# Gate and up products in one group per 512 features, with Strassen's seven products for three of eight pairs of row blocks

## The chip, the core and the metric

One core of a Trainium2 chip runs the kernel. The metric is the device time of one execution in microseconds (us). Before the change it is 1198.21 us, the median of 3 runs (1197.5 to 1198.28).

## What is computed

One encoder layer on 256 tokens of width 2048, all in 32-bit floats:

```python
u = rms_norm(h, g_mix_pre) @ w_in                       # 2048 x 5120
...                                                     # attention heads and RG-LRU heads
h = h + rms_norm(mixed, g_mix_post)
fn = rms_norm(h, g_ffn_pre)
ff = (silu(fn @ w_ffn_gate) * (fn @ w_ffn_up)) @ w_ffn_down   # 2048 x 5632, twice; 5632 x 2048
h = h + rms_norm(ff, g_ffn_post)
gate = sigmoid(rms_norm(h, g_ple_pre) @ w_ple_gate)     # 2048 x 2048
h = h + rms_norm(gate * (p @ w_ple_proj), g_ple_post)
```

The change concerns the line with `ff`: the two products of `fn` with the gate and the up weights.

## The kernel before

**Products.** A product of two 32-bit matrices is made of three matmuls. Each operand is split into a rounded high part and the rest, and high x high, high x low and low x high are added up in PSUM (lines 390, 391 and 392 of `products`). Weights come from DRAM as tiles `wr` of two row blocks (2 x 128 rows) by 512 columns, 512 KB each. ScalarE (ACT) writes the high part `wh` of a tile (`hi_stream`, line 362) and VectorE (DVE) the low part `wl` = `wr` - `wh` (`lo_stream`, line 372). TensorE (PE) then uses the tile for both halves of the tokens (t = 0, 1): 2 row blocks x 2 halves x 3 = 12 matmuls of 128 x 128 by 512 columns. The stationary operand is the transposed activation (`hT_mix_hi`, `hT_mix_lo`), one 128 x 128 block for each row block and token half.

**Segments and posts.** `seg` lists one chunk of 512 output columns. `run_seg` runs its tiles on PE into two PSUM banks (`acc`, a ring of four), and the chunk's `post` empties them. For each of the 11 blocks of 512 features there is a gate chunk (8 tiles), whose post `gate_post` lets ACT write silu into `mid`, and an up chunk (8 tiles), whose post `up_post` multiplies on DVE (line 1194), transposes the result on PE (line 262) and splits it (lines 243 and 245). The features are done in three parts of 4, 4 and 3 blocks, and after each part come four chunks of the down product. The residual `h` stays in SBUF from the mixing sub-layer to the end.

**Order.** `Plan` writes the program out in a fixed order. It holds an estimated clock for ACT, DVE, PE and the DMA queue, and with `run` it hands out the tasks that can start before PE's clock; every engine later works through its own list strictly in that order and waits on semaphores. How many weight tiles can be ahead of PE is set by the rings: `W_BUFS` = 4 split tiles, `R_BUFS` = 4 raw tiles. All loads go through the SP queue.

Of the kernel before, what the change touches and what calls it, by code (L numbers as in the profile page):

```python
# [16 lines left out]
P = 128  # L17
# [35 lines left out]
W_BUFS = 4  # L53
R_BUFS = 4
SM_BUFS = 4
LATE = 0.8

# [12 lines left out]
class Plan:  # L70
# [13 lines left out]
    def __init__(self, **slots):  # L84
        self.clk = {"act": 0.0, "dve": 0.0, "pe": 0.0, "dma": 0.0}
# [90 lines left out]
    def main(self, cost, *after):  # L176

        t = max([self.clk["pe"]] + [self.reach(e) for e in after])
        self.clk["pe"] = max(t, self.clk["pe"]) + cost
# [18 lines left out]

def dma(kb, take=None):
    return ("dma", kb / 340.0, None, take, None)  # L200
# [3 lines left out]
def layer(ctx: ExitStack, tc: tile.TileContext, a: dict, out: bass.AP):  # L204
# [5 lines left out]
    plan = Plan(wr=R_BUFS, w=W_BUFS, sm=SM_BUFS, ev=1, mid=2, bt=2)  # L210
# [4 lines left out]
    def bank(name):  # L215
        return ps.tile([P, 2, S], F32, tag="sm", name=name, bufs=SM_BUFS)

    def raw_tile():
        return wp.tile([P, 2, N], F32, tag="wr", name="wr", bufs=R_BUFS)

# [34 lines left out]
    def transposed(e, b0):  # L255

        yield pe(0.44, take="sm")
        tr = bank("tr")
        for b in range(2):
            for t in range(NT):  # L260
                sl = slice((b0 + b) * P, (b0 + b + 1) * P)
                nc.tensor.transpose(tr[:, b, t * P : (t + 1) * P], e[:, t, sl], ident)  # L262
        return tr
# [26 lines left out]
    class Act:  # L290


        def __init__(self, blocks=KD):
            self.at = {}
# [24 lines left out]

    raws, his, los = {}, {}, {}  # L320
# [4 lines left out]
    def pieces(i):  # L325

        return [slice(0, 1), slice(1, 2)] if i == 0 else [slice(0, 2)]

    def load_stream():
        for i, (w, k, n0) in enumerate(tiles):  # L330
            for j in pieces(i):
# [5 lines left out]
                if not j.start:  # L337
                    raws[i] = raw_tile()
# [3 lines left out]
    at_hi, at_lo, at_pe = [0], [0], [0]  # L342
# [5 lines left out]
    def hi_stream():  # L348
        for i in range(len(tiles)):
            at_hi[0] = i  # L350
            for j in pieces(i):
# [4 lines left out]
                yield act(n * N, take=None if j.start or i in big_w else "w")  # L356
                if i in big_w:
                    his[i], los[i] = big_w[i][0](), big_w[i][1]()
                elif not j.start:
                    his[i] = wp.tile([P, 2, N], F32R, tag="wh", name="wh")  # L360
                    los[i] = wp.tile([P, 2, N], F32R, tag="wl", name="wl")
                nc.scalar.copy(his[i][:, j, :], raws[i][:, j, :])  # L362
                done(ev_hi[i, j.stop])

    def lo_stream():
        for i in range(len(tiles)):
            at_lo[0] = i
            for j in pieces(i):
                n = j.stop - j.start
                yield ev_hi[i, j.stop]  # L370
                yield dve(n * N, give="wr" if j.stop == 2 else None)
# [5 lines left out]
            raws.pop(i)  # L377

    MM = 0.216

    def products(i, kx, lhs, accs, ts, start, stop, *after):
        for j in range(2):
            here = ev_lo[i, j + 1] if (i, j + 1) in ev_lo else ev_lo[i, 2]
            plan.main(6 * MM * len(ts) / NT, here, lhs.ev[kx + j], *after)
# [12 lines left out]

    def free_w(i):
        if i not in keep:
            plan.free["w"].append(plan.clk["pe"])  # L400

    keep = set()
    opened = []

    def open_chunk(chunk):
        if len(opened) >= 2:
            plan.reach(opened[-2].free)
        opened.append(chunk)
        chunk.accs = [ps.tile([P, N], F32, tag="acc", name=f"acc{t}") for t in range(NT)]

    def run_seg(s):
# [5 lines left out]
        for n, (_, kx) in enumerate(ks):  # L417
            i = i0 + n
            before = [opened[-3].free] if first and n == 0 and len(opened) > 2 else []
            products(i, kx, lhs, chunk.accs, range(NT), first and n == 0,  # L420
                     last and n == len(ks) - 1, *before)
# [153 lines left out]
    def evac(ch, func, tables):  # L575
# [8 lines left out]
        done(ch.free)  # L584
# [297 lines left out]
    def v_post(g):  # L882
        def post(ch):
# [14 lines left out]
            done(ch.free)  # L898
# [74 lines left out]
    def open_p2():  # L973
# [5 lines left out]
        for n in ("h", "mg", "ple"):  # L979
            t2[n] = rs.tile([P, NT, D], F32, name=n)  # L980
        t2["pTh"] = rs.tile([P, 2, S], F32R, name="pTh")
        t2["pTl"] = rs.tile([P, 2, S], F32R, name="pTl")
        t2["pw"] = rs.tile([P, 2, S], F32, name="pw")
        plan.add(load_p2(), plan.clk["pe"])

    pT = Act(2)
    ev_h = Event()
# [8 lines left out]
    def load_p2():  # L996
# [6 lines left out]
        for t in range(NT):  # L1003
            yield dma(1024)
            nc.sync.dma_start(t2["h"][:, t, :], a["x"][t * P : (t + 1) * P, :])
# [6 lines left out]
    class Sub:  # L1012
# [10 lines left out]
        def chunk(self, c, ch, add=False):  # L1023
# [28 lines left out]
            done(ch.free)  # L1052
# [9 lines left out]
        def squares(self, c, t, src, ev):  # L1062
            yield act(N)
            junk = t2["pool"].tile([P, N], F32, tag="junk", name="junk", bufs=2)
# [7 lines left out]
    def next_norm(sub, nxt, rstd, ev_rstd, g_next):  # L1072
# [11 lines left out]
        plan.add(next_gain(g_next, plan.now), plan.now)  # L1084
        yield ev_h
# [4 lines left out]
        for c in range(4):  # L1090
            if c > 1:
                yield nxt.ev[4 * c - 8]
            for b in range(2):
                sl = slice(c * N + b * S, c * N + (b + 1) * S)
                for t in range(NT):
                    yield dve(S)
                    nc.vector.scalar_tensor_tensor(
                        out=h[:, t, sl], in0=mg[:, t, sl], scalar=ro[:, t : t + 1],
                        in1=h[:, t, sl], op0=ALU.mult, op1=ALU.add,
# [3 lines left out]
        for c in range(4):  # L1103
            sl = slice(c * N, (c + 1) * N)
            for t in range(NT):
                yield act(N)
                junk = t2["pool"].tile([P, N], F32, tag="junk", name="junk", bufs=2)
                nc.scalar.activation(junk, h[:, t, sl], AF.Square, accum_out=ssh[:, t, c : c + 1])
# [4 lines left out]
        done(ev_rstd)  # L1113

# [4 lines left out]
    def transpose_h(b, hi, lo, nxt, gname):  # L1119
        tr = yield from transposed(t2["h"], b)  # L1120
        for j in range(2):
            kk = b + j
            yield from gained_split(
                hi[:, kk, :], lo[:, kk, :], tr[:, j, :], col(gname, kk), give="sm" if j else None
            )
            done(nxt.ev[kk])


    def ple_post(c):
        def post(ch):  # L1130
            for t in range(NT):
                yield act(N)
                nc.scalar.copy(t2["ple"][:, t, c * N : (c + 1) * N], ch.accs[t])
            done(ch.free)
# [40 lines left out]
    def gate_post(f):  # L1175
        def post(ch):
            yield ev_rf
            for t in range(NT):
                yield act(N, SILU, take=None if t else "mid")
                if t == 0:  # L1180
                    es[f] = t2["pool"].tile([P, NT, N], F32, tag="mid", name="mid", bufs=2)
                nc.scalar.activation(
# [243 lines left out]
```

## Time and profile before

| what | value |
|---|---|
| median of the runs | 1198.21 us |
| span of the profiled execution (first to last instruction) | 1195.1 us |
| PE busy in that span | 1176.7 us, 5388 matmuls |
| DVE busy | 695.1 us |
| ACT busy | 635.0 us |
| DMA traffic | 232.23 MB, mean 194 GB/s |

The page gives no separate time for the profiled execution. Its span is 3.1 us below the median of the runs; that difference is what lies around the span. Read the table from the top: PE's row says how much of the span the products alone take, the rows of DVE and ACT how much room is left beside them.

### The profile page before, as it was taken

How to read it: one execution, taken by the hardware profiler on the slowest of the kernel's cores; microseconds unless marked ns; L12 is line 12 of the kernel's file. 1: busy time of each engine (PE TensorE's matmuls, PEld its weight loads, DVE VectorE, ACT ScalarE, POOL GpSimd, SP SyncE). 2: the span in 40 equal slices, each digit the busy share in tenths (PEclk: the TensorE clock that was granted, in tenths of full speed). 3: DMA queues.
4: the chain of work that ended last, by engine and by line, in shares of the span. 5: the costliest groups of instructions: out<-in, count | busy, mean ns of one | idle time of the engine just before them, and what ended most of it. 6: DMA issues, size and time to landing. Idle time of an engine off the chain costs nothing.

```text
span 1195.1 us, 14294 instructions
## 1 busy us (share of the span) xinstructions
PE 1176.7 (98%) x5388; PEld 975.7 (82%) x5388; DVE 695.1 (58%) x823; ACT 635.0 (53%) x842; POOL 1.6 (0%) x13
## 2 busy tenths in 40 slices
PE   7999999999999999999999999999999999999996
PEld 5888888888888888888888888888888888888885
DVE  5676867877557545545444544545454544657664
ACT  6787776766457344344444444443334444446753
POOL 0000000000000000000000000000000000000000
PEclk9999999999999999999999999999999999999998
DMA  8765566545865666566666566565666666565661
GB/s 305 234 213 186 154 197 188 172 160 183 314 196 195 191 193 183 190 193 187 193 194 193 186 193 191 184 194 187 193 194 194 189 184 194 175 208 177 218 222 72
DMA packets 69205, 232.23 MB, mean 194 GB/s; under 512 B 7440, under 2 KB 13456, under 8 KB 68496
## 3 DMA queue, kind: packets, MB, share of 16 engines
q1 hardware_dynamic: 68992, 231.24, 61.2%
q8 instruction: 42, 0.69, 0.2%
q14 instruction: 27, 0.22, 0.1%
q10 hardware_dynamic: 144, 0.08, 0.0%
HBM read 229.19 MB, written 2.10 MB: 194 GB/s over the span
## 4 chain that ended last, share of the span: by engine, by line
PE 98%; DVE 1%; ACT 0%; DMA 0%; SPq 0%; issue 0%; DVEq 0%
PE acc L392 31%; PE acc L390 31%; PE acc L391 31%; PE tr L262 2%; DMA xs<-in_xT 0%; PE pg L267 0%; PE pg L268 0%; PE pg L266 0%; PE tr L877 0%; DVE wl L372 0%; DVE h L1310 0%; PE po L268 0%; PE sc L267 0%; PE sc L268 0%; PE po L267 0%; PE po L266 0%
## 5 line engine op out<-in xcount | busy, mean ns | idle before, releaser
L372 DVE TENSOR_TENSOR wl<-wr,wh 128x1024 fp32r<-128x1024 f32 (+1 forms) x409 | 497.2, 1221 | 379.4 <-ACT wh L362 379.1
L362 ACT CAST wh<-wr 128x1024 fp32r<-128x1024 f32 (+1 forms) x409 | 428.7, 1050 | 471.5 <-PE acc L392 451.5
L390 PE MATMUL acc<-wh,hT_mix_hi 128*128 128x512 f32 x704 | 275.8, 392 | 0.0
L392 PE MATMUL acc<-wh,hT_mix_lo 128*128 128x512 f32 x704 | 274.3, 390 | 0.3 <-DVE hT_mix_lo L251 0.3
L391 PE MATMUL acc<-wl,hT_mix_hi 128*128 128x512 f32 x704 | 274.0, 389 | 0.0
L392 PEld LDWEIGHTS acc<-wh,hT_mix_lo 128*128 128x128 f32 x704 | 132.1, 188 | 28.5 <-DVE hT_mix_lo L251 0.9
L391 PEld LDWEIGHTS acc<-wl,hT_mix_hi 128*128 128x128 f32 x704 | 132.2, 188 | 26.9
L390 PEld LDWEIGHTS acc<-wh,hT_mix_hi 128*128 128x128 f32 x704 | 132.2, 188 | 26.6
L390 PE MATMUL acc<-wh,hT_hi 128*128 128x512 f32 x320 | 127.9, 400 | 6.9 <-ACT wh L362 6.9
L391 PE MATMUL acc<-wl,hT_hi 128*128 128x512 f32 x320 | 125.7, 393 | 1.4 <-DVE wl L372 1.4
L392 PE MATMUL acc<-wh,hT_lo 128*128 128x512 f32 x320 | 125.5, 392 | 0.0
L390 PEld LDWEIGHTS acc<-wh,hT_hi 128*128 128x128 f32 x320 | 60.6, 189 | 18.5 <-ACT wh L362 6.9
L391 PEld LDWEIGHTS acc<-wl,hT_hi 128*128 128x128 f32 x320 | 60.4, 189 | 14.7 <-DVE wl L372 3.2
L392 PEld LDWEIGHTS acc<-wh,hT_lo 128*128 128x128 f32 x320 | 60.3, 189 | 12.9
L390 PE MATMUL acc<-wh,mid0h 128*128 128x512 f32 x128 | 50.0, 390 | 0.0
L390 PE MATMUL acc<-wh,mid1h 128*128 128x512 f32 x128 | 50.0, 390 | 0.0
L392 PE MATMUL acc<-wh,mid0l 128*128 128x512 f32 x128 | 49.8, 389 | 0.0
L392 PE MATMUL acc<-wh,mid1l 128*128 128x512 f32 x128 | 49.8, 389 | 0.0
L391 PE MATMUL acc<-wl,mid0h 128*128 128x512 f32 x128 | 49.8, 389 | 0.0
L391 PE MATMUL acc<-wl,mid1h 128*128 128x512 f32 x128 | 49.8, 389 | 0.0
L390 PE MATMUL acc<-wh,hT_ffn_hi 128*128 128x512 f32 x112 | 44.1, 394 | 0.0
L392 PE MATMUL acc<-wh,hT_ffn_lo 128*128 128x512 f32 x112 | 43.7, 390 | 0.0
(231 smaller groups left out, 1308.4 us busy)
## 6 DMA issues: line engine op xcount, KB each, us to landing
wr<-in_w_ffn_gate SPq DMA_DIRECT2D x88, 512.0 KB, 4.2
wr<-in_w_ffn_up SPq DMA_DIRECT2D x88, 512.0 KB, 4.2
wr<-in_w_ffn_down SPq DMA_DIRECT2D x88, 512.0 KB, 4.3
wr<-in_w_in SPq DMA_DIRECT2D x79, 512.0 KB, 4.3
wr<-in_w_out SPq DMA_DIRECT2D x32, 512.0 KB, 4.6
wr<-in_w_ple_gate SPq DMA_DIRECT2D x32, 512.0 KB, 4.2
xn<-in_x SPq DMA_DIRECT2D x4, 512.0 KB, 6.2
h<-in_x SPq DMA_DIRECT2D x2, 1024.0 KB, 8.1
```

The source lines that it names most:

```text
L262: nc.tensor.transpose(tr[:, b, t * P : (t + 1) * P], e[:, t, sl], ident)
L362: nc.scalar.copy(his[i][:, j, :], raws[i][:, j, :])
L372: nc.vector.tensor_tensor(out=los[i][:, j, :], in0=raws[i][:, j, :], in1=f32(his[i][:, j, :]), op=ALU.subtract,)
L390: nc.tensor.matmul(accs[t], hi[:, sl], wh[:, j, :], start=st, stop=False)
L391: nc.tensor.matmul(accs[t], hi[:, sl], wl[:, j, :], start=False, stop=False)
L392: nc.tensor.matmul(accs[t], lo[:, sl], wh[:, j, :], start=False, stop=sp)
```

## The change

**One group for gate and up.** For each block of 512 features the two chunks become one `Group`. It goes through the eight pairs of row blocks once, and at each pair uses the gate tile and the up tile. So it needs four banks at once: `c11`, `c21` (gate, the two token halves) and `c12`, `c22` (up).

**Plain and Strassen units.** `KINDS` = "ppspspsp" says how each pair is done: "p" is plain (two tiles, 24 matmuls), "s" is done by seven products. The first group uses `FIRST` = "ppppspsp", with two "s". In a unit "s" the 2 x 2 block product (two row blocks; two token halves; gate and up) is done by seven block products of three matmuls each, 21 in all. Three of these products add straight into `c11`, `c12` and `c21`; four have banks of their own (`p1`, `p5`, `p6`, `p7`) in which all "s" units of a group add up.

**Sums.** Seven products need sums of the operands. For the activations (`act_sums`) they are made once, for row block pairs 4, 8 and 12, and kept in `sums_f`. For the weights (`sum_stream`) DVE makes two sum tiles per unit from the raw gate and up tiles, four subtractions of 128 x 512; they lie in `lent_t`, which has two places. The sum tiles are then split into high and low like raw tiles. Of the up tile only the second row block is split. So a unit "s" splits three and a half tiles where a unit "p" splits two.

**After the products** (`Gated`): `early` runs after the last "s" unit: ACT copies `p1`, DVE makes four additions from `p6`, `p5`, `p7`, `p5`. `late` runs at the group's end: four additions of DVE onto `c11`, `c21`, `c12`, `c22`, then silu, product, transposes and split as before. The two rings of four banks, `acc` and `sm`, change roles from group to group: one holds `c..`, the other `p..`, and the transposes of `late` take their banks in the ring of the old `c..`.

**Room.** `W_BUFS` goes from 4 to 6, one more split tile follows in the second half (`W_MORE`), and `h` is lent: after its norm it is written to DRAM (`kept0`, `kept1`, 1 MB each), its place serves as one more split tile (`lent_w`) and two more raw tiles (`lent_r`), and it is read back after the last group. The place of the gain serves as `lent_t`. Besides, `junk` gets one buffer, `sg` shares the buffers of `mid`, and the planner's estimate of a matmul goes from 0.216 to 0.2267.

```diff
-W_BUFS = 4
+W_BUFS = 6
...
+MM = 0.2267
...
+FIRST = "ppppspsp"
+KINDS = "ppspspsp"
...
+    def sum_stream():
+        for i, (i0, n) in sums.items():
...
+            a_, b_ = raws[i0], raws[i0 + 1]
+            yield dve(N, take="ts")
+            raws[i] = t = from_slot("ts", i)
...
+            first = b_[:, 0, :] if not n else b_[:, 1, :]
+            minus = a_[:, 0, :] if not n else raws[i - 1][:, 0, :]
+            nc.vector.tensor_tensor(out=t[:, 0, :], in0=first, in1=minus, op=ALU.subtract)
+            yield dve(N)
+            first = b_[:, 1, :] if not n else a_[:, 1, :]
+            minus = b_[:, 0, :] if not n else t[:, 0, :]
+            nc.vector.tensor_tensor(out=t[:, 1, :], in0=first, in1=minus, op=ALU.subtract)
...
+    FORMS = (
+        ("p1", 0, 0, (0, 0)), ("c11", 0, 1, (1, 0)), ("c12", 1, 1, 3), ("p5", 2, 0, 0),
+        ("p7", 2, 1, 2), ("p6", 3, 0, 1), ("c21", 3, 1, (1, 1)),
+    )
...
+    def seven(i, kx, g, start, stop):
+        for name, v, j, which in FORMS:
+            n = i + v
...
+            own = name[0] == "p"
+            at = g.take(name) if own and start else 0.0
+            plan.main(3 * MM, ev_lo[n, 2], ev, at=at)
+            times3(g.banks[name], hi, lo, his[n][:, j, :], los[n][:, j, :],
+                   own and start, own and stop)
...
+        def early(self, g):
...
+            nc.scalar.copy(e[:, 0, :], bk["p1"])
...
+            nc.vector.tensor_tensor(out=e[:, 1, :], in0=bk["p6"], in1=e[:, 0, :], op=ALU.add)
...
+            nc.vector.tensor_tensor(out=u[0], in0=bk["p5"], in1=e[:, 1, :], op=ALU.add)
...
+            nc.vector.tensor_tensor(out=e[:, 1, :], in0=bk["p7"], in1=e[:, 1, :], op=ALU.add)
...
+            nc.vector.tensor_tensor(out=u[1], in0=bk["p5"], in1=e[:, 1, :], op=ALU.add)
...
+        def late(self, g):
...
+            for t, n, x in (
+                (0, "c11", e[:, 0, :]), (1, "c21", e[:, 1, :]), (0, "c12", u[0]), (1, "c22", u[1]),
+            ):
+                yield dve(N)
+                nc.vector.tensor_tensor(out=x, in0=bk[n], in1=x, op=ALU.add)
...
+    def lend_h(h):
...
+            nc.sync.dma_start(t2["kept"][t], h[t])
...
+    def give_back():
+        yield ev_back["w"]
+        yield ev_back["wr"]
...
+            nc.sync.dma_start(t2["h"][t], t2["kept"][t])
...
         for f in range(f0, f1):
-            g = Chunk(gate_post(f))
-            seg(g, "w_ffn_gate", f * N, hF, KS)
-            seg(Chunk(up_post(f, mid, (f - f0) * 4, g)), "w_ffn_up", f * N, hF, KS)
+            Group(("w_ffn_gate", "w_ffn_up"), (f * N, f * N), hF,
+                  [(k, k) for k in ORDER], KINDS if f else FIRST, Gated(mid, (f - f0) * 4))
```

**How the order changes.** Three places matter for the steps below. In the names, a number tells tiles of one name apart.

VectorE's list before, where the post of an up chunk falls (the third block of features): between two posts there stand only splits of weight tiles.

```order
L372 TENSOR_TENSOR wl_4118<-wr_4061,wh_4117 128x1024
L372 TENSOR_TENSOR wl_4136<-wr_4073,wh_4135 128x1024
L372 TENSOR_TENSOR wl_4154<-wr_4091,wh_4153 128x1024
L1194 SCALAR_TENSOR_TENSOR mid_4024<-acc0_4016,rstd_f_92,mid_4024 128x512
L1194 SCALAR_TENSOR_TENSOR mid_4024<-acc1_4017,rstd_f_92,mid_4024 128x512
L372 TENSOR_TENSOR wl_4175<-wr_4109,wh_4174 128x1024
L245 TENSOR_TENSOR mid0l1_4191<-tr_4185,mid0h1_4190 128x512
L372 TENSOR_TENSOR wl_4195<-wr_4127,wh_4194 128x1024
```

VectorE's list now, at the end of `late` of the second group, while PE goes through the first units of the third group (the last row, `wl_4051`, is the low part of the second sum tile of that group's first "s" unit):

```order
L1513 SCALAR_TENSOR_TENSOR mid_3920<-u_lo_3933,rstd_f_94,mid_3920 128x512
L482 TENSOR_TENSOR lent_w_3414<-lent_r_3415,lent_w_3414 128x1024
L506 TENSOR_TENSOR lent_t_3127<-lent_r_3415 128x512
L291 TENSOR_TENSOR mid0l0_3662<-tr_4002,mid0h0_3661 128x512
L482 TENSOR_TENSOR wl_3936<-lent_r_3415,wh_3935 128x512
L502 TENSOR_TENSOR lent_t_3127<-lent_r_3415,lent_t_3127 128x512
L482 TENSOR_TENSOR wl_4017<-lent_t_3127,wh_4016 128x1024
L291 TENSOR_TENSOR mid0l0_3662<-tr_4027,mid0h0_3661 128x512
L506 TENSOR_TENSOR lent_t_3127<-lent_r_3415,lent_t_3127 128x512
L502 TENSOR_TENSOR lent_t_3127<-wr_3985,wr_3962 128x512
L506 TENSOR_TENSOR lent_t_3127<-wr_3985 128x512
L482 TENSOR_TENSOR wl_4051<-lent_t_3127,wh_4050 128x1024
```

The splits of `late`, the subtractions for the sums (lines 502 and 506) and the splits of weight tiles now stand between each other; `wl_4051` stands behind two subtractions that belong to the next "s" unit.

PE's list now, at the end of the eleventh group, where the down chunk takes the two `acc` banks that `c11` and `c21` of this group held:

```order
L523 MATMUL c12_7876<-wh_8089,hT_mix_lo_3129 128x512
L521 MATMUL c22_7877<-wh_8089,hT_mix_hi_3128 128x512
L522 MATMUL c22_7877<-wl_8090,hT_mix_hi_3128 128x512
L523 MATMUL c22_7877<-wh_8089,hT_mix_lo_3129 128x512
L521 MATMUL acc0_8197<-wh_8101,mid2h0_7554 128x512
L522 MATMUL acc0_8197<-wl_8102,mid2h0_7554 128x512
```

VectorE's list before those two banks come free (lines 1484 to 1493 are `early`, line 1506 is `late`):

```order
L1484 TENSOR_TENSOR mid_8155<-p6_7981,mid_8155 128x512
L1488 TENSOR_TENSOR u_hi_8171<-p5_7969,mid_8155 128x512
L1490 TENSOR_TENSOR mid_8155<-p7_7974,mid_8155 128x512
L1493 TENSOR_TENSOR u_lo_8172<-p5_7969,mid_8155 128x512
L482 TENSOR_TENSOR wl_8161<-wr_8127,wh_8160 128x1024
L482 TENSOR_TENSOR wl_8176<-wr_8135,wh_8175 128x1024
L1506 TENSOR_TENSOR mid_8155<-c11_7853,mid_8155 128x512
L1506 TENSOR_TENSOR mid_8155<-c21_7854,mid_8155 128x512
```

Before the change PE went here from an up chunk to two other banks of the ring, which had been empty for a whole chunk; now the first two banks of the down chunk come free with the last two rows.

The SP queue now, in the first group: the two stores of `h` stand between the loads of plain tiles and the loads of the last "s" unit, which land in `h`'s place.

```order
L432 DMA wr_3341<-in_w_ffn_gate 128x1024
L432 DMA wr_3356<-in_w_ffn_up 128x1024
L1328 DMA kept0_3387<-h0_2694 128x2048
L1328 DMA kept1_3388<-h1_2695 128x2048
L432 DMA lent_r_3415<-in_w_ffn_gate 128x1024
L432 DMA lent_r_3415<-in_w_ffn_up 128x1024
```

What moved: all later loads stand behind these stores, and the two `lent_r` loads also wait until the stores have read `h`.

More of the change, by code (lines that the diff above doesn't have):

```diff
@@ L1132, in post @@
                 yield act(N)
[L1133 to L1134 removed]
+                nc.scalar.copy(ple_of(c)[:, t, :], ch.accs[t])
+            release(ch)
         return post
@@ L1326, in layer @@
                 ev[i, j.stop] = Event()
+    for i, (i0, n) in sums.items():
+        if not n:
+            for u in (i0, i0 + 1, i):
+                uses[u] += 1
     i0 = segs[-1][-1]
```

421 lines of the change are left out of this document (337 added, 84 removed).

## The prediction, made before the changed kernel was run

> **What bounds the kernel now.** I read the page first: busy times and the chain that ended last.
>
> ```profile
> span 1195.1 us, 14294 instructions
> PE 1176.7 (98%) x5388; PEld 975.7 (82%) x5388; DVE 695.1 (58%) x823; ACT 635.0 (53%) x842; POOL 1.6 (0%) x13
> ...
> PE 98%; DVE 1%; ACT 0%; DMA 0%; SPq 0%; issue 0%; DVEq 0%
> ```
>
> PE is busy 1176.7 of 1195.1 us and the chain is PE nearly from end to end. Next the list of waits, for PE alone, and the busy time from the first gate chunk to the middle of the FFN.
>
> ```profile
> PE acc L390 <- ACT wh L362: 6.9, 1, 6.9
> PE acc L391 <- DVE wl L372: 1.4, 2, 0.7
> PE acc L392 <- DVE hT_mix_lo L251: 0.3, 1, 0.3
> ...
> 360.00:728.00 368.00, 368.00 (x1657) 304.72 (x1656) 187.18 (x182) 167.69 (x195) 0.00 (x0) 1.00 0.62 191
> ```
>
> Columns of the last row: the stretch, its length, then busy time (and count) of PE, PEld, DVE, ACT, POOL, PE's granted clock, the DMA share and GB/s. PE waited 8.6 us in all, 6.9 of them for its first weights, and in the FFN not at all: 368.00 of 368.00 us, at clock 1.00. DVE is at 187.18 (51%). So there a matmul less is time less, as long as DVE, which gets much more work, keeps ahead.
>
> The price of a matmul is not its duration (they overlap) but the distance of starts:
>
> ```profile
> 700.31 0.39 PE L390 MATMUL acc<-wh,hT_mix_hi 128*128 128x512 f32 x1
> ...
> 705.75 0.39 PE L390 MATMUL acc<-wh,hT_mix_hi 128*128 128x512 f32 x1
> ...
> 540.14 0.44 PE tr L262 x4
> ```
>
> These two starts are 24 matmuls apart: 5.44 / 24 = 0.2267 us. Four transposes take 0.44.
>
> **What PE saves.** Each "s" unit has 21 matmuls for 24. There are 2 in the first group and 3 in each of ten: 32 x 3 = 96 matmuls less, 96 x 0.2267 = 21.8 us. A group takes PE 183 x 0.2267 + 2 x 0.44 = 42.4 us (before: 192 x 0.2267 + 0.88 = 44.4). [...]
>
> **What DVE and ACT get.** DVE's rows (duration in ns at the end of the busy column), ACT's and the DMA's:
>
> ```profile
> L372 DVE TENSOR_TENSOR wl<-wr,wh 128x1024 fp32r<-128x1024 f32 x407 | 495.8, 1223 | 379.4 <-ACT wh L362 379.1
> L1194 DVE SCALAR_TENSOR_TENSOR mid<-acc,rstd_f,mid 128x512 f32<-128x512 f32 x22 | 15.4, 744 | 0.0
> L1279 DVE TENSOR_TENSOR sg<-sg,ple 128x512 f32<-128x512 f32 x8 | 5.5, 688 | 11.9 <-ACT sg L1275 11.9
> L1232 DVE TENSOR_TENSOR mg<-acc,mg 128x512 f32<-128x512 f32 x8 | 5.1, 683 | 0.0
> ...
> L362 ACT CAST wh<-wr 128x1024 fp32r<-128x1024 f32 x407 | 427.5, 1052 | 471.5 <-PE acc L392 451.5 <-DMA wr<-in_w_out 5.1 <-issue 4.9
> L1182 ACT ACTIVATE mid<-acc,rstd_f 128x512 f32<-128x512 f32 x22 | 15.0, 690 | 9.9 <-PE acc L392 9.9
> L1229 ACT COPY mg<-acc 128x512 f32<-128x512 f32 x8 | 4.7, 589 | 4.3 <-PE acc L392 3.9
> ...
> wr<-in_w_ffn_gate SPq DMA_DIRECT2D x88, 512.0 KB, 4.2
> ...
> h<-in_x SPq DMA_DIRECT2D x2, 1024.0 KB, 8.1
> ```
>
> A group of five "p" and three "s" has on DVE: splits of 128 x 1024: 5 x 2 + 3 x 3 = 19; pieces of 128 x 512: 3 (half tiles) + 12 (sums) + 4 (`early`) + 4 (`late`) + 2 (splits of `mid`) = 25; 2 of line 1194's kind. By durations (L1279 and L1232 for the pieces, 0.69): 19 x 1.223 + 25 x 0.69 + 2 x 0.744 = 42.0 us. That would be PE's 42.4, with nothing to spare. But do durations add up? The timeline of DVE where it is dense:
>
> ```profile
> 362.31 1.22 DVE L372 TENSOR_TENSOR wl<-wr,wh 128x1024 fp32r<-128x1024 f32 x1
> 363.44 0.48 DVE L1097 SCALAR_TENSOR_TENSOR h<-mg,ro_mix,h 128x256 f32<-128x256 f32 x1
> ...
> 408.33 0.69 DVE L245 TENSOR_TENSOR mid0l<-tr,mid0h 128x512 fp32r<-128x512 f32 x1 [1.98 <-ACT mid0h L243]
> 408.94 1.22 DVE L372 TENSOR_TENSOR wl<-wr,wh 128x1024 fp32r<-128x1024 f32 x1
> ...
> 448.03 1.40 DVE L1194 SCALAR_TENSOR_TENSOR mid<-acc,rstd_f,mid 128x512 f32<-128x512 f32 x2
> ...
> 1123.12 0.69 DVE L1279 TENSOR_TENSOR sg<-sg,ple 128x512 f32<-128x512 f32 x1 [0.78 <-ACT sg L1275]
> 1123.85 0.69 DVE L1284 TENSOR_TENSOR mg<-sg,gain_g_ple_post 128x512 f32<-128x512 f32 x1
> ```
>
> The first columns are start and length. A next instruction starts 1.13 us after a split of 1.22, 0.61 after a piece of 0.69, 0.66 (1.40 - 0.74) after line 1194's; only where it uses the result of the one just before (L1284 after L1279) is it 0.73. So a group costs DVE 19 x 1.13 + 25 x 0.61 + 2 x 0.66 = 38.0, and about 12 dependent pairs (`early`, sums, `late`) x 0.12 = 1.4: 39.4 us, 93% of PE's 42.4. ACT has 19 x 1.05 + 3 x 0.59 + 0.59 + 2 x 0.69 + 2 x 0.59 = 24.9 us: room. Loads are the same 16 tiles per group, 8.4 MB in 42.4 us, 198 GB/s against 191 in the row above; they and the loads' issue stay hidden behind split tiles, of which seven or eight can now be ahead of PE (19 us of plain tiles at 2.72).
>
> [...]
>
> **New waits of PE, one by one.**
>
> First, the second sum tile of a group's first "s" unit. In the list shown, `wl_4051` stands behind the whole of `late`. From the group's start, DVE has up to it the four additions, 2 of line 1194's kind, 4 splits of 1024 and 8 pieces more: 12 x 0.61 + 2 x 0.66 + 4 x 1.13 = 13.2 us, with 8 dependent pairs 14.1; by durations 14.7. PE needs it after two "p" units, two transposes and five products: 48 x 0.2267 + 0.88 + 15 x 0.2267 = 15.2 us. It holds by 0.5 to 1.1 us, if no cast of ACT (1.05) that DVE waits for is exposed. One exposed in each of ten groups would cost up to 0.5 us each, two 1.6. I take 0.2 on average, 2 us; ends 0 and 16.
>
> Second, the banks. `early` has the 5.44 us of the last "p" unit: ACT's copy 0.59 and four dependent additions of 0.73 are 3.5 us. It holds by 1.9, more than one split (1.13) in the way. Then, from one group to the next, the banks of `c..` need only be free for the next "s" unit, 11 us later. But at the end of the eleventh group the down chunk takes the banks of `c11` and `c21` at once: 3.5 + two splits 2.26 + one addition 0.61 = 6.4 us after the last "s" unit, against 5.44: PE waits 1.0 us there, once. Ends 0 and 4 (ACT's copy late by one cast, three splits more). After the fourth and the eighth group the down chunk takes what were banks of `p..`, free since `early`: nothing.
>
> Third, `h` to DRAM. The last "s" unit of the first group comes 117 matmuls, 26.5 us, after the last transposes of `h`. Before its sums can be made, the SP queue must reach the stores (behind a tile whose place comes free some 6.5 us after the last rows of `h`, by DVE's list), the stores must land (8.1 us as for the two loads of `h`, if they overlap; 16.2 if not), the tiles must land (4.2), then four subtractions (2.9), a cast (1.05) and a split (1.2). That is 24 or 32 us against 26.5 plus 2 us until the first sum is used. I take 1 us, nearer the overlapped case since both loads of `h` show 8.1 with weights between them; ends 0 and 4. Coming back, `h` has the 65 us of the last down chunks: nothing. If that cover went, next late would be the norm before the PLE gate.
>
> Other edits cost nothing, all hidden behind a PE that is 98% busy: the sums of the activations (three times about 1.6 us of DVE and ACT, in the 26 us after the norm, where the first four units are plain), the one buffer of `junk` (written by ACT alone, in order), `sg` in `mid`'s place (no `mid` lives then), the larger rings. Unchanged: the start (6.9 + 1.4 us in the rows of waits) and the tail:
>
> ```profile
> 1100.00:1195.00 95.00, 85.28 (x382) 70.18 (x381) 58.52 (x76) 53.52 (x87) 0.00 (x0) 0.96 0.51 167
> ```
>
> 9.7 us of it without PE: ACT, DVE and the last stores.
>
> **Sum.** 1195.1 - 21.8 + 2 + 1 + 1 = 1177.3 us of span; with the 3.1 us around it (median 1198.2 less span) 1180.4 us, 1.5% faster.
>
> **Rivals.**
>
> *DVE paces the groups.* If durations add up (42.0) and the list adds one or two waits for ACT per group (the copy of `p1`, the casts behind the transposes; 1.05 each, say 1.4), a group takes 43.4 and not 42.4: 11 us more over eleven groups, 1180.4 - 2 (the first wait is in it) + 11 = 1189 us. For it: DVE at 93 to 99% leaves no room for a list in a fixed order. Against: the starts quoted, and seven or eight split tiles that bridge a local lag.
>
> *The sum ring turns DVE's list into a ping-pong* (the other side). `lent_t` has two places: DVE subtracts, ACT casts, DVE splits, and only then does DVE subtract for the next unit. If DVE stands through the cast at each of the six sum tiles of a group, 6 x 1.05 = 6.3 us come on top of 39.4: 45.7 for 44.4 before, 11 x 1.3 = 14 us slower, 1198 + 14 + 2 = 1214. It decides from 5.0 us of exposed waits per group on (44.4 - 39.4). Row L372 shows that DVE does wait for casts, 379.4 us in all. Against: there it had nothing else to do; in the new list other splits stand between most subtractions and the split of the sum.
>
> *Nothing happens*: PE not the limit in the FFN. The stretch of 368 us excludes it; only a chance meeting of gain and waits could give no change.
>
> **How the numbers follow.** The forecast (1176.4 with no wait to about 1184 with the upper halves of the three waits) 0.70; DVE paces (1184 to 1196, at 1189) 0.18; ping-pong 0.07; gain and waits within 0.2% of each other, which is about what a measurement of this kernel tells from no change, 0.03; something lower than 1176, a shorter start by the larger rings, 0.02. So faster 0.90, same 0.03, slower 0.07. For 8 in 10 the range holds the forecast and the nearer part of DVE's pacing: 1175 to 1190.
>
> **What would show it.** Right: PE has 5292 matmuls, its starts still 0.2267 apart; waits of PE in the groups sum to a few us, on `p6` products, `acc` of the first down chunk after the eleventh group and the last "s" unit of the first group; DVE some 90% busy there. DVE pacing: PE waits for `wl` in every group, 1 us each, DVE without idle. Ping-pong: DVE's idle before the splits of `lent_t` put down to ACT, six times a group. Wrong altogether: matmuls further apart than 0.2267 because one engine's reads hinder another's, which no stretch of this trace can show.

## The result and the profile after

The changed kernel takes 1180.88 us (median of 4 runs, 1180.2 to 1181.52) against 1198.24 us in the same measurement (4 runs, 1197.5 to 1198.6): 0.9854 of the time before, 95% interval 0.984 to 0.9868, 17.4 us less. 1180.4 was predicted.

The page of after, the lines that answer to those of before: span and busy times, and the head of the chain that ended last.

```profile
span 1179.4 us, 14527 instructions
PE 1159.9 (98%) x5292; PEld 959.8 (81%) x5292; DVE 878.8 (75%) x1118; ACT 686.9 (58%) x925; POOL 1.6 (0%) x13
...
PE 87%; DVE 6%; DMA 3%; ACT 2%; issue 1%; SPq 1%; DVEq 0%; ACTq 0%
```

5292 matmuls are 96 fewer than 5388. PE still spans 98%, and DVE went from 58 to 75%. All of PE's waits after, and then the same two stretches of the FFN in both kernels (columns as in the prediction), after first:

```profile
PE acc L521 <- ACT wh L457: 6.4, 1, 6.4
PE acc L522 <- DVE wl L482: 1.7, 1, 1.7
PE acc L521 <- DVE mid L1506: 0.5, 1, 0.5
PE pg L314 <- DVE xcl L291: 0.4, 2, 0.2
```

```profile
360.00:728.00 368.00, 367.75 (x1657) 303.43 (x1656) 299.37 (x369) 206.30 (x256) 0.00 (x0) 1.00 0.62 200
450.00:492.00 42.00, 42.00 (x190) 34.77 (x190) 39.27 (x48) 23.80 (x28) 0.00 (x0) 1.00 0.65 203
```

```profile
450.00:492.00 42.00, 42.00 (x191) 34.79 (x190) 19.83 (x18) 18.03 (x19) 0.00 (x0) 1.00 0.61 191
```

In these 42 us PE does not stand in either kernel, while DVE's time doubles, from 19.83 to 39.27: 94% busy, and still no wait of PE. (Over the longer stretch PE stands for 0.25 of 368 us after.)

Where the 15.7 us between the two spans (1195.1 and 1179.4) come from, by the starts of three matmuls in each trace: the first gate product of the FFN, the first down product of its third part, and the end.

| stretch | before | after | difference |
|---|---|---|---|
| span's start to the FFN's first product | 357.3 | 361.6 | +4.3 |
| FFN up to the third part's first down product | 665.3 | 644.8 | -20.5 |
| rest | 172.5 | 173.0 | +0.5 |

So the FFN gave the whole gain, and the part ahead of it, whose products the change leaves as they are, lost a fifth of it. The experiments ask how far DVE was from setting the time, and where the 4.3 us went.

### The profile page after: what moved, and what is told of

It is laid out like the page before. It is cut to its first block, busy times and chain, and to the rows that moved or that the text cites. A ratio compares the mean times of both kernels' runs of the same rounds, so it can differ in the third digit from the quotient of the medians.

```text
span 1179.4 us, 14527 instructions
## 1 busy us (share of the span) xinstructions
PE 1159.9 (98%) x5292; PEld 959.8 (81%) x5292; DVE 878.8 (75%) x1118; ACT 686.9 (58%) x925; POOL 1.6 (0%) x13
## 4 chain that ended last, share of the span: by engine, by line
PE 87%; DVE 6%; DMA 3%; ACT 2%; issue 1%; SPq 1%; DVEq 0%; ACTq 0%
PE acc L523 17%; PE acc L522 17%; PE acc L521 17%; PE c L521 7%; PE c L522 7%; PE c L523 7%; DVE wl L482 2%; PE p L531 2%; PE p L532 2%; PE p L530 2%; PE c L530 2%; PE c L532 2%; PE c L531 2%; PE tr L309 2%; DMA av<-in_w_rg_i 1%
## 5 line engine op out<-in xcount | busy, mean ns | idle before, releaser
L482 DVE TENSOR_TENSOR wl<-wr,wh 128x1024 fp32r<-128x1024 f32 (+1 forms) x322 | 375.9, 1182 | 145.0 <-ACT wh L457 144.3
L457 ACT CAST wh<-wr 128x1024 fp32r<-128x1024 f32 (+1 forms) x322 | 323.5, 1020 | 221.8 <-PE acc L523 135.3
L521 PE MATMUL c<-wh,hT_mix_hi 128*128 128x512 f32 x400 | 157.3, 393 | 0.0
L523 PE MATMUL c<-wh,hT_mix_lo 128*128 128x512 f32 x400 | 155.8, 390 | 0.0
L522 PE MATMUL c<-wl,hT_mix_hi 128*128 128x512 f32 x400 | 155.8, 389 | 0.0
L523 PEld LDWEIGHTS c<-wh,hT_mix_lo 128*128 128x128 f32 x400 | 75.1, 188 | 16.0 <-DVE hT_mix_lo L297 0.2
L521 PEld LDWEIGHTS c<-wh,hT_mix_hi 128*128 128x128 f32 x400 | 75.1, 188 | 15.1
L522 PEld LDWEIGHTS c<-wl,hT_mix_hi 128*128 128x128 f32 x400 | 75.2, 188 | 15.0
L482 DVE TENSOR_TENSOR wl<-lent_r,wh 128x1024 fp32r<-128x1024 f32 (+1 forms) x58 | 64.4, 1118 | 22.2 <-ACT wh L457 22.1
L457 ACT CAST wh<-lent_r 128x1024 fp32r<-128x1024 f32 (+1 forms) x58 | 55.4, 969 | 41.7 <-PE acc L523 25.0
L482 DVE TENSOR_TENSOR wl<-lent_t,wh 128x1024 fp32r<-128x1024 f32 x56 | 66.9, 1218 | 10.6 <-ACT wh L457 10.5
```

The source lines that it names most:

```text
L482: nc.vector.tensor_tensor(out=los[i][:, j, :], in0=raws[i][:, j, :], in1=f32(his[i][:, j, :]), op=ALU.subtract,)
L521: nc.tensor.matmul(accs[t], hi[:, sl], wh[:, j, :], start=st, stop=False)
L522: nc.tensor.matmul(accs[t], hi[:, sl], wl[:, j, :], start=False, stop=False)
L523: nc.tensor.matmul(accs[t], lo[:, sl], wh[:, j, :], start=False, stop=sp)
```

## The experiments

All times below are medians; the kernel before gave 1197.7 to 1198.3 us beside them, and a ratio is always to it.

**How many "s" units: one, and four.** The first edit leaves one "s" unit in each group, the second makes four (and gives the place of one split tile to the fourth sum of the activations).

```diff
-FIRST = "ppppspsp"
-KINDS = "ppspspsp"
+FIRST = "pppppspp"
+KINDS = "pppppspp"
```

> One 's' unit in each group instead of three (two in the first): 11 units of seven products instead of 32, so 21 units x 3 = 63 more matmuls, 5355 in all. If PE alone sets the time of a group (the theory), 63 x 0.2267 = 14.3 us more than the changed kernel: 1195.2 us, and 33 matmuls fewer than before with the start as in the changed kernel. If DVE held the groups back or the reads of the sums slowed PE (rival), taking away two thirds of DVE's extra work would give part of that back: 1185 to 1190 us.

Measured: 1195.11 us (ratio 0.9973, 0.9961 to 0.9984). The price of a matmul, 0.2267 us, holds for 63 of them, so PE set the time of the groups with three "s" as well, to within the 1 us that the medians scatter. DVE, in the same 42 us, with one "s":

```profile
450.00:492.00 42.00, 42.00 (x191) 34.79 (x190) 30.86 (x34) 20.06 (x22) 0.00 (x0) 1.00 0.57 189
```

```diff
-W_MORE = 1
-FIRST = "ppppspsp"
-KINDS = "ppspspsp"
+W_MORE = 0
+FIRST = "pppppssp"
+KINDS = "pspspssp"
```

> Four 's' units in each group but the first (which keeps two), and one split tile less since the place of a fourth sum of the activations is taken from it. PE saves 10 x 3 x 0.2267 = 6.8 us more: 1174 us if PE still sets the time (rival). DVE's distance of starts went from 30.6 us a group with one 's' to 38.1 with three, 3.8 for each: 41.9 with four, and with the 4.4 us that it stood waiting for casts in the groups of the run with the doubled subtractions 46.3 us against PE's 41.7. In that run seven of eleven groups showed it: 7 x 4.6 = 32 us more than PE's time, 1206 us, and some us more for the slower clock after the waits (the theory).

Measured: 1201.8 us (1.0036, 1.0022 to 1.005): 21 us slower than with three, although PE has 30 matmuls less. PE's waits in it:

```profile
PE p L531 <- DVE wl L482: 6.5, 9, 0.8
PE p L530 <- ACT wh L457: 5.5, 7, 1.0
```

About 1206 was expected. These are the waits of the prediction's two rivals, and the next pair of runs shows how they come about.

**A little more work for DVE.** In both kernels subtractions of the sums are made again, with the same values to the same place, once per "s" unit in the first and, by the edit below, more often in the second.

```diff
+            for _ in range(1 - n):        # second kernel: range(2 - n)
+                yield dve(N)
+                nc.vector.tensor_tensor(out=t[:, 0, :], in0=first, in1=minus, op=ALU.subtract)
```

> One of the four subtractions of each 's' unit is done a second time: three more instructions of 128 x 512 on DVE in a group. By the distance of starts (0.61 each) DVE goes from 39.4 to 41.2 us a group and stays under PE's 42.4: 0 to 2 us slower than the changed kernel, 1181 to 1183. By durations (0.69 each, 42.0 a group already) it goes to 44.1, 1.7 over PE in each of eleven groups: about 19 us slower, 1200.

Measured: 1185.13 us (0.9892, 0.9873 to 0.9911), 4.2 us more than the changed kernel. Durations that add up (1200) are excluded; the sum of starts was right in kind and 2 to 4 us short. Of the three waits below, those of the second and the fourth group are where the prediction put its first one, at the second sum tile of a group's first "s" unit; that of the first group is another (the third of the prediction, see the point on it):

```profile
PE p L534 <- DVE wl L482: 2.4, 3, 0.8
```

> The same subtraction twice more: six more instructions on DVE in a group than the changed kernel. By the distance of starts DVE then takes 39.4 + 6 x 0.61 = 43.1 us, plus about 3 x 2 x 0.12 where one waits for the one before, 43.8: 1.4 over PE's 42.4, and about 15 us slower than the changed kernel, 1196. By durations 42.0 + 6 x 0.69 = 46.1: 41 us slower, 1222.

This expectation counted the edit wrongly: two sums per unit give 2 + 1 more, so nine instructions a group and not six. By starts that is 9 x 0.61 = 5.5 us on top of the 38.6 that a group costs DVE after the change (see the point on DVE's load), 44.1 for PE's 42.4, 1.7 x 11 = 19 us more, 1200 us. Measured: 1224.29 us (1.0218, 1.02 to 1.0236), 43 us more. One of its groups, as a window and as DVE's group of splits of the sums (the last columns: idle time before them and what ended it):

```profile
459.00:507.00 48.00, 44.69 (x189) 35.33 (x188) 43.53 (x56) 22.39 (x27) 0.00 (x0) 0.96 0.54 173
```

```profile
L482 DVE TENSOR_TENSOR wl<-lent_t,wh 128x1024 fp32r<-128x1024 f32 x5 | 6.1, 1225 | 2.9 <-ACT wh L457 2.9
```

DVE is busy 43.5 of 48 us and stands for 4.5, 2.9 of them before splits of sums. That is the ping-pong of the prediction's second rival, seen singly in its timeline and in that of PE (start, length, engine, line; in brackets the wait):

```profile
425.64 0.69 DVE L509 TENSOR_TENSOR lent_t<-wr,lent_t 128x512 f32<-128x512 f32 x1
427.50 1.23 DVE L482 TENSOR_TENSOR wl<-lent_t,wh 128x1024 fp32r<-128x1024 f32 x1 [1.16 <-ACT wh L457]
```

```profile
426.10 0.39 PE L535 MATMUL p<-wh,sums_f 128*128 128x512 f32 x1
427.52 0.69 PE L533 MATMUL p<-wh,sums_f 128*128 128x512 f32 x1 [1.03 <-ACT wh L457]
428.78 0.79 PE L534 MATMUL p<-wl,sums_f 128*128 128x512 f32 x1 [0.57 <-DVE wl L482]
429.37 0.63 PE L535 MATMUL p<-wh,sums_f 128*128 128x512 f32 x1
429.80 0.63 PE L533 MATMUL c<-wh,hT_mix_hi 128*128 128x512 f32 x1
430.22 0.63 PE L534 MATMUL c<-wl,hT_mix_hi 128*128 128x512 f32 x1
```

DVE makes the last subtraction, ACT casts, DVE splits, and PE stands through both. And there is a second price: after three waits PE's matmuls are 0.43 apart (429.37, 429.80, 430.22) where they were 0.2267, without waiting for anything, and the granted clock reads 0.50 there (last section). In six of the eleven groups seven to twelve matmuls are that slow, 1.4 to 2.4 us. So a late DVE costs more than its lateness. By the starts of the groups' first products, six of the eleven take 48.8 us and not 42.4 (38 us in all), the first one 3.5 more, and the first two after a stretch of down chunks at most 0.3 more: there DVE had got ahead.

**The planner's price of a matmul.** The one number MM = 0.2267 goes back to 0.216.

```diff
-MM = 0.2267
+MM = 0.216
```

> The changed kernel planned with the old estimate of a matmul, 0.216. Theory M: first gate product at about 357.3 us, and up to 4.3 us faster unless the FFN, planned with too fast a PE, loses it again. Theories R and T: the part before the FFN as in the changed kernel; in the FFN the lists give DVE's work in another order, 0 to 3 us of waits more: 1180.9 to 1184 us.

Measured: 1187.54 us (0.9916, 0.9902 to 0.993), 6.7 us worse than the changed kernel. That the new price of a matmul costs the time before the FFN is refuted: there this run is slower still (the FFN starts at 366.3, in an execution that was the slowest of six, 1192.23 us). In the FFN waits appear at the two sum tiles of the first "s" unit, as with more work for DVE:

```profile
PE p L531 <- DVE wl L482: 1.9, 3, 0.8
...
PE p L530 <- ACT wh L457: 1.2, 3, 0.6
...
PE p L531 <- DVE lent_w L482: 0.8, 1, 0.8
```

A plan that thinks PE faster than it is puts the steps in another order, and a margin of about 1 us at the sum tiles does not survive that; which of the moved steps does it was not tested.

**Fewer places for split tiles ahead of the FFN.** First the changed kernel with four split tiles up to the mixing sub-layer, three more from there on (as many in the FFN as before); then the kernel before with six; then the first again, but with all six places set aside from the start and two of them not used until then, so that its lists are those of the first and its tiles lie as in the changed kernel.

```diff
-W_BUFS = 6
+W_BUFS = 4
-W_MORE = 1
+W_MORE = 3
```

> The changed kernel with 4 split tiles before the FFN (as in the kernel before) and 3 more in the second half, so the FFN keeps its eight. Theory R (the larger ring reorders the lists before the FFN and that costs the 4.3 us by which the changed kernel came late to its first gate product): the first gate product comes at about 357.3 us, the time is 1176.6 us. Theory T (the first loads land at other moments from execution to execution, and PE's slow clock at the start multiplies it): the first 22 us are the same list, so the start stays anywhere between that of the two kernels, and only the 1.2 us of waits between 50 and 250 us may go: 1179.7 to 1180.9 us. Theory M (the planner's 0.2267 in place of 0.216 reorders the part before the FFN): no change there, 1180.9 us.

Measured: 1179.15 us (0.9842, 0.9829 to 0.9855), between the figures of theory R (1176.6) and of theory T (1179.7 to 1180.9), and nearer the second.

```diff
-W_BUFS = 4
+W_BUFS = 6
-    nc = bacc.Bacc("TRN2", target_bir_lowering=False, num_devices=1)
+    nc = bacc.Bacc("TRN2", target_bir_lowering=False, num_devices=1, dynamic_dma_scratch_size=1024)
```

> The kernel before with 6 split tiles in place of 4, and the smaller scratch area that makes room for it. Theory R: first gate product at about 361.6 us and 1202.5 us. Theory T: 1198.2 us, within 1 us. Theory M: 1198.2 us.

Measured: 1202.26 us (1.0032, 1.002 to 1.0043). Here theory R was right. The scratch size is that of the changed kernel. The run with the later rings has that scratch size as well, and its FFN began at 357.9 us against 357.3 in the kernel before; so it is the larger ring that makes the kernel before 4 us slower.

```diff
+W_FIRST = 4
-        wr=R_BUFS, w=W_BUFS, ts=0, acc=ACC_BUFS, sm=SM_BUFS, ev=1, mid=2, bt=2, uv=1
+        wr=R_BUFS, w=W_FIRST, ts=0, acc=ACC_BUFS, sm=SM_BUFS, ev=1, mid=2, bt=2, uv=1
+    held = w_slots[W_FIRST:]
+    del w_slots[W_FIRST:]
...
+        for x in held:
+            w_slots.append(x)
+            plan.free["w"].append(plan.clk["pe"])
```

> All six places for split tiles are set aside from the start, as in the changed kernel, but the plan uses only four of them up to the mixing sub-layer and all from there on: each engine's list is word for word that of the run with four places, only the place of the tiles in SBUF is that of six. If the order of the lists with six places loses the time before the FFN, this one has the start of the run with four (hundredth matmul at 33.9 us, 1179.2 us). If the place of the tiles or the landing of the first loads that goes with it does it, the start is that of the changed kernel (hundredth matmul at 36.4 us) and the time about 1181 to 1182.

Measured: 1180.34 us (0.9849, 0.9834 to 0.9864). Its start lies between the two that were expected (hundredth product at 34.6 us), so this run does not decide between the order and the place.

**PE's clock at the start.** The timeline of PE, before and then after, around its first long wait:

```profile
9.94 0.57 PE L390 MATMUL acc<-wh,hT_hi 128*128 128x512 f32 x1
11.18 0.50 PE L391 MATMUL acc<-wl,hT_hi 128*128 128x512 f32 x1 [0.67 <-DVE wl L372]
11.51 0.39 PE L392 MATMUL acc<-wh,hT_lo 128*128 128x512 f32 x1
11.74 0.39 PE L390 MATMUL acc<-wh,hT_hi 128*128 128x512 f32 x1
```

```profile
9.72 0.80 PE L521 MATMUL acc<-wh,hT_hi 128*128 128x512 f32 x1
12.25 0.79 PE L522 MATMUL acc<-wl,hT_hi 128*128 128x512 f32 x1 [1.73 <-DVE wl L482]
12.84 0.63 PE L523 MATMUL acc<-wh,hT_lo 128*128 128x512 f32 x1
...
17.96 0.60 PE L523 MATMUL acc<-wh,hT_lo 128*128 128x512 f32 x1
18.39 0.41 PE L521 MATMUL acc<-wh,hT_hi 128*128 128x512 f32 x1
18.64 0.40 PE L522 MATMUL acc<-wl,hT_hi 128*128 128x512 f32 x1
```

Before, matmuls are 0.23 apart from 11.5 us on; after, the wait is longer and they stay 0.43 apart until 18.4: twelve more at that distance, 2.4 us. The record of the granted clock in the two traces begins with a change to 1.00, at 10.31 us before and at 18.40 us after. The next two kernels give PE something to do there.

```diff
+    idle = bank("idle")
+
+    def turn(count):
+        for _ in range(count):
+            nc.tensor.matmul(idle[:, 0, 0:P], ones, ones, start=True, stop=True)
...
+                if (i, j, t) == (0, 1, 0):
+                    turn(5)
                 nc.tensor.matmul(accs[t], hi[:, sl], wl[:, j, :], start=False, stop=False)
...
+        turn(11)
         for n, s in enumerate(segs[:-1]):
```

> The changed kernel with 16 more matmuls of 128 x 128 by 128 columns on a constant, into a bank nobody reads: 11 ahead of PE's first product, while PE waits for its first weights, and 5 at the place of PE's first long wait (after the seventh matmul). If the time before the FFN is lost because PE's clock rises late (matmuls 0.427 apart until 18.4 us in the changed kernel, until 9.5 in the kernel before), they keep PE busy and the clock rises early: no matmul 0.427 apart after 11 us, the hundredth matmul at 33.5 us instead of 36.1, and 1178 to 1179 us. If the loads land late and the clock only follows (rival), the hundredth matmul stays at 36 us and the time at 1181.

Measured: 1180.19 us (0.9851, 0.9836 to 0.9866). Its PE at the start:

```profile
1.13 4.54 PE L440 MATMUL idle<-ones 128*128 128x128 f32 x22 [1.13 <-POOL ones L273]
6.75 0.50 PE L526 MATMUL acc<-wh,hT_hi 128*128 128x512 f32 x1 [1.08 <-ACT wh L462]
...
8.96 1.27 PE L440 MATMUL idle<-ones 128*128 128x128 f32 x10
11.10 0.50 PE L529 MATMUL acc<-wl,hT_hi 128*128 128x512 f32 x1 [0.86 <-DVE wl L487]
11.44 0.39 PE L530 MATMUL acc<-wh,hT_lo 128*128 128x512 f32 x1
```

The mechanism is as expected: no slow product at all, and the hundredth one at 33.1 us instead of 36.1. But the median fell by only 0.7 us, which the scatter of these runs does not tell from nothing.

> The same 16 matmuls in the kernel with four split tiles up to the mixing sub-layer. Its clock rose by 10.0 us in the profiled execution; if that is the rule for it, nothing changes: 1179.2 us, hundredth matmul at 33.6. If it was luck of that execution and others of it rise late, the median falls by 0.5 to 1.5 us: 1177.7 to 1178.7.

Measured: 1180.3 us (0.9853, 0.9837 to 0.9869; its four runs lie between 1178.23 and 1182.74). No gain. Here PE was at full pace from its first product and its hundredth came only at 34.4 us, with one wait at 9.85 us of 2.56 us from start to start, behind which ACT and DVE wait for the loads of `xs`.

So the start has two sources of chance: the clock's rise (10.31 us before, 18.40 after) and the landing of the first loads (of the loads issued in the first 5 us, the two of 512 KB landed 5.8 us after their issue before and 6.9 after, in the median). All profiled executions, one of each kernel, by the starts of PE's products (the matmuls on the constant not counted):

| kernel | split tiles ahead of the mixing sub-layer | hundredth | of them 0.43 apart | FFN's first | between the two |
|---|---|---|---|---|---|
| before | 4 | 33.4 | 4 | 357.3 | 323.9 |
| later rings | 4 | 33.6 | 4 | 357.9 | 324.3 |
| two held | 4 | 34.6 | 15 | 359.8 | 325.2 |
| later rings, clock kept up | 4 | 34.4 | 0 | 359.0 | 324.6 |
| later rings, h not lent | 4 | 33.5 | 4 | 359.0 | 325.6 |
| after | 6 | 36.1 | 16 | 361.6 | 325.5 |
| after, clock kept up | 6 | 33.1 | 0 | 359.4 | 326.3 |
| one "s" | 6 | 34.4 | 11 | 361.4 | 327.0 |
| four "s" | 6 | 33.9 | 4 | 362.6 | 328.7 |
| subtractions repeated, first kernel | 6 | 35.0 | 15 | 362.3 | 327.3 |
| subtractions repeated, second kernel | 6 | 33.8 | 11 | 360.7 | 326.9 |
| h not lent | 6 | 34.8 | 8 | 362.2 | 327.4 |
| before with six | 6 | 35.9 | 15 | 363.8 | 327.9 |
| MM = 0.216 | 6 | 36.6 | 15 | 366.3 | 329.7 |

The last column does not follow the two columns of the start. By the traces the compute instructions of PE, ACT and DVE ahead of the FFN (up to 310 us at least) stand in only four different orders, set by the number of places and by the planner's price of a matmul:

| places, price | kernels | between the two | mean |
|---|---|---|---|
| 4, 0.216 | before | 323.9 | 323.9 |
| 4, 0.2267 | the other four with 4 | 324.3 to 325.6 | 324.9 |
| 6, 0.2267 | after and six more | 325.5 to 328.7 | 327.0 |
| 6, 0.216 | before with six, MM = 0.216 | 327.9, 329.7 | 328.8 |

So two more places cost 2.1 us in the means at the changed kernel's price. The kernel before with six loses more, in an order that is not the changed kernel's. The changed kernel's own 1.6 us over the kernel before is a single execution of an order that scatters by 3 us. PE's waits there are small steps: with six places and 0.2267 for transposes near 50 us (six of the seven executions) and for the gates near 154 and 193 us, in the kernel before with six for `attn_hi` near 270 us. That work made further ahead is what holds these steps up is argued and not shown. In the time of the changed kernel four places instead of six are not clear of the scatter either: 1179.15 and 1180.34 against 1180.88, with the clock kept up 1180.3 against 1180.19, without the lending (below) 1178.46 against 1180.42. The first part, hundredth product at 33.1 to 36.6, scatters within either number of places.

**h not lent.** The store, the reload and the lent places go; the FFN has seven split tiles and four raw ones.

```diff
-                plan.add(give_back(), plan.now)
...
-    ev_hs = {"mix": ev_h, "ffn": ev_h2}
+    ev_hs = {"mix": ev_h, "ffn": ev_h}
...
-        if n == "mix":
-            plan.add(lend_h(h), plan.now)
```

> h is not lent: no store and no reload of 2 MB, and in the FFN 7 split tiles and 4 raw tiles instead of 8 and 6. If the split tiles ahead are reserve enough (the theory), the lending was worth little: 1180 to 1183 us. If the raw tiles are what DVE's sums wait for, since each sum holds two raw tiles until both subtractions are done (rival), DVE stands in every group and PE waits 1 to 2 us in each: 1192 to 1203 us.

Measured: 1180.42 us (0.9852, 0.9838 to 0.9867), the same as with h in DRAM. The lending brings nothing that can be measured. It moves a wait: without it the one in the first group is gone, and PE waits 1.3 us at the second sum tile of the fourth group's first "s" unit.

**Both simplifications**: four split tiles ahead of the FFN, and h not lent (the two diffs above together).

> Both simplifications together: four split tiles up to the mixing sub-layer (the run with the later rings gave 1179.15 us) and h not lent (1180.42 us, against 1180.88 with it). If the part from the hundredth matmul to the FFN is 324 to 325 us with the lists of four split tiles, as in the three runs that had them, and the FFN needs no lent place, 1178.5 to 1179.8 us and no more than 1.5 us of waits in the groups. If seven split tiles that come only with the mixing sub-layer, without the eighth from h, leave too little ahead (rival), waits at the first 's' units of the groups of 1 us each, 1181 to 1184 us.

Measured: 1178.46 us (5 runs, 1178.22 to 1180.97; 0.9841, 0.9827 to 0.9855). All its waits of PE:

```profile
PE acc L520 <- ACT wh L456: 7.1, 1, 7.1
PE acc L521 <- DVE wl L481: 1.4, 2, 0.7
PE pg L314 <- DVE xcl L291: 0.8, 1, 0.8
PE p L530 <- DVE wl L481: 0.8, 1, 0.8
```

The first two are the start and like those of before; one is left in the gates and one in the groups (the fourth, as without the lending alone). It has the lowest median of all, 2.4 us under the changed kernel, but the intervals of the two ratios overlap: shown is that the simpler kernel is not slower.

## Why the prediction was right, point by point

**PE's saving** (96 x 0.2267 = 21.8). Right, shown by the run with one "s" (63 matmuls, 14.3 us expected and 14.2 measured) and by the FFN's 20.5 less. A group without a wait takes 42.4 us in the trace, as summed: the distance of starts did not change, so the fear of matmuls that run further apart for other engines' reads fell away.

**DVE's load** (39.4 us a group by starts, or 42.0 by durations). The starts were right to 0.8 us: from one `early` to the next (486.40 to 528.83 us) DVE has a group's 46 instructions and is busy 38.6 us. In the new list, splits and pieces close together:

```profile
465.82 0.68 DVE L502 TENSOR_TENSOR lent_t<-wr,lent_t 128x512 f32<-128x512 f32 x1
466.42 1.22 DVE L482 TENSOR_TENSOR wl<-wr,wh 128x1024 fp32r<-128x1024 f32 x1
467.55 0.69 DVE L506 TENSOR_TENSOR lent_t<-wr,lent_t 128x512 f32<-128x512 f32 x1
468.16 1.82 DVE L482 TENSOR_TENSOR wl<-wr,wh 128x1024 fp32r<-128x1024 f32 x2
```

A piece of 0.68 is followed after 0.60, a split of 1.22 after 1.13. The durations of those 46 instructions add up to 41.7 us; with the 3.8 us that DVE stands in the same stretch that is 45.5, more than the 42.4 that it took. "DVE paces" as the prediction priced it (durations add) was therefore the wrong mechanism; but a DVE that paces was near: 1.8 and 5.5 us more of it per group cost 4.2 and 43 us.

**First wait, the second sum tile** (2 us taken, ends 0 and 16). None: in the profiled execution PE stands at no such tile in any of the ten groups, so the margin of 0.5 to 1.1 us held there. With three more instructions of DVE a group, with four "s" units, with MM = 0.216, and once in the kernels without the lending, it is among the waits that appear, 1 us or a little more a time.

**Second wait, the banks after the eleventh group** (1.0). Right: 0.91 - 0.23 = 0.7 us, once.

```profile
1005.51 0.39 PE L523 MATMUL c<-wh,hT_mix_lo 128*128 128x512 f32 x1
1006.42 0.47 PE L521 MATMUL acc<-wh,mid2h 128*128 128x512 f32 x1 [0.52 <-DVE mid L1506]
```

**Third, h to DRAM** (1). The place was right: PE's one wait at a sum tile is at the first sum of the last "s" unit of the first group, 0.44 - 0.23 = 0.2 us. The SP queue, ACT and PE in that order:

```profile
378.73 0.91 SPq L1328 DMA_DIRECT2D kept<-h  x2
388.82 0.33 SPq L432 DMA_DIRECT2D lent_r<-in_w_ffn_gate  x1
...
392.47 1.05 ACT L457 CAST lent_w<-lent_r 128x1024 fp32r<-128x1024 f32 x1 [5.28 <-DMA lent_r<-in_w_ffn_gate]
...
398.66 0.39 PE L530 MATMUL p<-wh,sums_f 128*128 128x512 f32 x1
399.10 0.50 PE L531 MATMUL p<-wl,sums_f 128*128 128x512 f32 x1
```

The loads start 10.1 us after the stores, nearer the overlapped case (8.1) than the other (16.2), and ACT stands for them. The 0.2 us is a small draw: of the four other kernels with the same groups, three (later rings, two held, after with the clock kept up) wait 0.7 to 1.1 us there and one 0.3; the two without the lending do not wait there. The lending was not needed. The waits in the FFN came to 1.2 us (21.76 - 20.52) and not 4: the 0.2 here, the 0.7 above and smaller bits.

**The larger rings at no cost, and "Unchanged: the start".** This step failed. The FFN began 4.3 us later. The two profiles split it: 2.8 us lie in the first hundred products, where the clock rose late, which other runs do not all show, and 1.6 us between the hundredth product and the FFN. Of the second part the order of the lists with six places explains 2.1 us in the means of the runs (the kernel before with six is 4 us slower); in the changed kernel's time it is not clear of the scatter. The prediction had called the rings hidden "behind a PE that is 98% busy"; but a larger ring changes in what order PE, ACT and DVE work, and that is not hidden where PE waits for the work that came later.

**The sum.** "3.1 us around the span" was also two things: in every run measured since, time less span is 1.8 us (1181.19 and 1179.4 for after). The profiled execution of before was thus itself 1.3 us faster than the median, with an early clock. So the sum, 1177.3 us of span, was met with 1179.4: 2.8 us too much for waits in the FFN, 4.8 too little for what lies outside it (4.3 ahead, 0.5 behind). The predicted 1180.4 lay within 0.5 us of the median because these two errors and the 1.3 nearly cancel, which is luck: the saving and the second wait were right, the first wait, the start and the time around the span were not.

## What to carry to other kernels

Where one engine is busy without a gap, its work can be cut by counting, at the distance of starts (63 matmuls: 14.3 us counted, 14.2 measured); what limits the cut is the next engine's list with its waits, which here was full at 38.6 of 42.4 us: one more "s" unit turned 17 us of gain into 4 us of loss. A larger ring is no free reserve under a planner, since it reorders work in parts of the program that were not touched (4 us in the kernel before): give the places only to the stage that needs them. And look at the first 20 us of a profile before reading a difference of 2 us into a change.

## What the hardware did that was not expected

A wait of PE can cost more than itself. After the waits in the groups with the repeated subtractions, and after the first long wait of eight of the 14 profiled executions, PE's matmuls of 512 columns started 0.427 us apart and not 0.2267, for 3 to 7 us. The granted clock (the third number from the end of a row) shows it, here around the waits of the timeline shown above:

```profile
424.24:427.65 3.41, 1.62 (x7) 0.99 (x6) 2.21 (x4) 1.23 (x2) 0.00 (x0) 1.00 0.10 13
430.00:432.00 2.00, 2.00 (x6) 1.52 (x6) 2.00 (x3) 0.83 (x2) 0.00 (x0) 0.50 0.88 246
```

The 0.96 over the whole group shown answers to about 4 us at half clock in 48 us (0.04 x 48 / 0.5 = 3.8). Only at the start does such a row mislead: ahead of the first change that a trace records (18.40 us after) it reads 1.00 although the products are 0.427 apart.

In the first of the two rows PE is busy for 1.62 of 3.41 us, and the clock still reads 1.00; in the second, behind it, it reads 0.50. Not every wait was followed by a slow stretch: after the 0.7 us that PE stood behind the eleventh group in the changed kernel, the products start 0.30, 0.24 and 0.23 us apart (from 1006.42 us on), and the clock from 1006 to 1010 us reads 1.00. Which waits cost extra is not shown.

The moment of the rise differs from trace to trace: the last product of the start that is followed only 0.42 or 0.43 us later begins at 9.52 us in the kernel before, 9.56 with the later rings, 17.96 in the changed kernel and 19.55 with MM = 0.216.
